# Six of nine pairs of adaLN modulations made as row dot products on VectorE, GpSimd and ScalarE

## The chip, the cores and the metric

One core of one Trainium2 chip runs the whole program once per launch. The metric is the device time of one execution in microseconds (us), the median of several runs. Three runs of the kernel before took 2188.8, 2191.82 and 2193.41 us.

## What is computed

A diffusion transformer of two layers for one image: 256 latent tokens `x` and 256 context tokens `h`, model width 1024, all float32. Each layer is a feed-forward half step, a mixer (layer 0: latent attention and a gated delta rule; layer 1: gated linear attention and windowed attention), and a second feed-forward half step. Shift, scale and gate of each of them come from the conditioning vector (adaLN): nine modulations per layer of width 1024, one set for the latents from `c`, one for the context from `c_ctx`.

```
sc, scc = silu(c), silu(c_ctx)
for i in range(2):
    mx = split(sc @ ada_w[i] + ada_b[i], 9)     # latents
    mh = split(scc @ ada_w[i] + ada_b[i], 9)    # context
    x = ffn_half_step(x, norm_g[i, 0], mx[0], mx[1], mx[2], ...)
    h = ffn_half_step(h, norm_g[i, 0], mh[0], mh[1], mh[2], ...)
    xn = modulate(rms_norm(x, norm_g[i, 1]), mx[3], mx[4])
    hn = modulate(rms_norm(h, norm_g[i, 1]), mh[3], mh[4])
    ox, oh = mixer_i(xn, hn, ...)
    x = x + mx[5] * ox
    x = ffn_half_step(x, norm_g[i, 2], mx[6], mx[7], mx[8], ...)
    if i == 0: the same for h with mh[5] to mh[8]
```

The matrices `ada_w` are 2 x 1024 x 9216 floats, 72 MB, and are used once, for two vectors. The 18 modulations are numbered m = 9 * layer + j; in layer 1 the context needs only m = 9 to 13.

## The kernel before

The tokens lie in columns: 8 tiles of 128 rows of the width by 256 tokens for each of the two sequences. Every weight block (128x1024, 512 KB) comes from DRAM through `fetch` (L216) on the SP queue into a ring of buffers `raw`; `halves` (L221) splits it into two parts of 11 bits, `whi` by a ScalarE cast (L224) and `wlo` by a VectorE subtraction with both operands in SBUF (L227), and `mm3` (L248) multiplies the three products that matter on TensorE. A feed-forward half step, `ffn` (L410), runs in four groups of 6, 6, 5 and 5 hidden tiles: for each tile a gate block and an up block of 24 matmuls each into a bank `f`, then `gated` (L464: `sg`, `ah`, `al`); at a group's end eight blocks of the down projection, whose results `add` (L475) puts onto the tokens (`x`, L405). `norm_h` (L374) makes the normed and modulated tokens (`hnf`, `hh`, `hl`) from modulations 3j and 3j + 1 of a step; the gate is needed first at group 0's end.

A pair of modulations is made by `ada` (L296). It is eight steps, one for each 128 rows of the width: two blocks of 512 KB are fetched, and four matmuls (eight records in the trace) with 32 stationary columns, of which two hold silu of `c_ctx` and `c`, run side by side into the four quarters of the bank `aux`. After the eighth step VectorE transposes the bank (`sqa`, L311) and adds the bias.

```
for q in range(2):
    r = 32 * (2 * e + q)
    self.mm(pb[r:r + 32, :], self.sc[:, k, :], raw[:, 512 * q:512 * q + 512], k == 0, k == NK - 1, cost=0.215)
```

`more_ada` (L324) does the next steps. It is called in `contexts` (L1674) before the first feed-forward step, for pair 0; in each tile of every `ffn` (L491), on that step's own ring of `raw`; and, if pairs are left, in the last mixer. All 72 steps were made within the first 1117 us.

The order of the work: streams of TensorE's work (feed-forward steps, mixer parts) are woven by their ranks (`weave`, L193) against a count of TensorE's time, and a scheduler then sets each engine's order by priority and its own estimate of when instructions are ready. Each engine executes its list in order; so does the SP queue, where a fetch waits until the block's buffer in its ring was read. The context's first step is `ffn00c`, then the latents' `ffn00x` beside the context's mixer, and so on; `ffn01x` and `ffn10x` are the latents' steps after the first mixer.

Of the kernel before, what the change touches and what calls it, by code (L numbers as in the profile page):

```python
# [83 lines left out]
def pack(i):  # L84
# [60 lines left out]
class Net:  # L145
# [75 lines left out]
    def halves(self, pool, raw, w, bufs, width=1024, ffn=False):  # L221
        """The part of 11 bits and what it leaves."""
# [40 lines left out]
    def setup(self):  # L263
# [16 lines left out]
        self.ada_gen, self.ada_pair = None, 0  # L280
# [15 lines left out]
    def ada(self, pair, pool, raws):  # L296
        """Modulations 2 pair and 2 pair + 1, one block of DRAM at each step."""
        nc = self.nc
        pb = self.bank("aux")
        for k in range(NK):  # L300
            pool, raws = self.ada_from
            for e in range(2):
                raw = self.fetch(pool, self.I["ada"][pair, k, :, 1024 * e:1024 * e + 1024], raws)
# [10 lines left out]
        for e in range(2):  # L314
            l, j = divmod(2 * pair + e, 9)
            v = self.mod[:, 2 * pair + e]
            if j % 3 == 1:
                g = self.ng[:, 3 * l + j // 3].unsqueeze(2).to_broadcast([128, NK, 2])
                nc.vector.scalar_tensor_tensor(v, v, 1.0, g, op0=ALU.add, op1=ALU.mult)
            elif j in (2, 8):  # L320
                nc.vector.tensor_scalar(v, v, 0.5, None, op0=ALU.mult)
        yield

    def more_ada(self, n, upto, pool, raws):  # L324
        """The next n blocks of the modulations' weights, no further than pair upto."""
        self.ada_from = pool, raws
        for _ in range(n):
            if self.ada_pair > min(upto, 8):
                return
# [80 lines left out]
    def ffn(self, l, j, s, side, name, rank, end=False, begin=None, raws=3, bufs=4, rows=8, tanh=False):  # L410
        """Streams of this kind share two banks: the one of lowest rank has them."""
# [21 lines left out]
        def run(ctx, pool, h):  # L433
            with ctx:
                yield 10.0
                yield from owned()
# [17 lines left out]
                def turn():  # L454
                    """Between two banks, where another stream may go first."""
# [25 lines left out]
                for lo, hi in GROUPS:  # L481
                    aT = []
                    for f in range(lo, hi):
# [6 lines left out]
                        n = NK * (f + 1) // 6 - NK * f // 6 if 2 * self.ada_pair <= gate else 1  # L490
                        self.more_ada(n, 8, pool, raws)  # L491
                        yield from turn()
                    while 2 * self.ada_pair <= gate:
                        self.more_ada(1, 8, pool, raws)
                    for k in range(0, NK, 2):
# [9 lines left out]
                        product(pb[:, N:2 * N], aT, hi - lo)  # L505
# [1222 lines left out]
```

## Time and profile before

| | |
|---|---|
| three runs | 2188.8, 2191.82, 2193.41 us |
| profiled execution: span of its instructions | 2186.0 us |
| TensorE busy / VectorE / ScalarE / GpSimd | 2102.0 / 1422.2 / 1072.3 / 241.2 us |
| `aux` matmuls of the modulations | 576 records, 111.4 us busy |
| bytes moved | 388.6 MB, mean 178 GB/s |
| first normed tile `hnf` of the context | 37.35 us |
| `ffn00c` | to 292 us |
| groups 0 and 1 of `ffn01x` | 1175 to 1281 us |

The profile was taken of one more execution; of its own time only the span from its first to its last instruction is given, 2186.0 us, 5.8 us below the median of the runs. Busy time counts an engine's instructions once where they overlap. A timeline row gives start, duration, engine, line, operation, result <- operands and shape; a bracket at its end tells how long the engine stood idle before it, and what ended that. PE is TensorE, PEld its weight loads, DVE is VectorE, ACT ScalarE, POOL GpSimd.

### The profile page before, as it was taken

Reading aid. Unit: us, or ns where it says so; the run is one execution under the profiler, and the core shown is the slowest. Engines: PE = TensorE matmul, PEld = TensorE weight load, DVE = VectorE, ACT = ScalarE, POOL = GpSimd, SP = SyncE. Lnnn points to the kernel's source line nnn. Section 1 sums busy time; section 2 is a strip of 40 time slices with the busy share of each in tenths; the row PEclk is TensorE's granted clock in tenths of the full one; section 3 lists DMA queues with packets and bytes.
Section 4 is the critical chain, followed back from the end, with each engine's and each line's share of the span. In section 5 each row is a group of like instructions: output and inputs, shape, how many; then the busy total and the mean of one; then the engine's idle time right before and its main releaser. Section 6 shows DMA issues by size and latency. Waiting matters only on the chain.

```text
span 2186.0 us, 45677 instructions
## 1 busy us (share of the span) xinstructions
PE 2102.0 (96%) x17688; PEld 1919.2 (88%) x17688; DVE 1422.2 (65%) x3153; ACT 1072.3 (49%) x2304; POOL 241.2 (11%) x496
## 2 busy tenths in 40 slices
PE   6999999999999989999998999999999998998999
PEld 2778888888898788887898999899999997878999
DVE  3545567886566878765576666766676766666665
ACT  3434456544434564444355555555555655435554
POOL 0000006601000175010000000100000001000000
PEclk8999999999999999999999999999999998999999
DMA  9867755665445645653356555555456552124554
GB/s 338 292 225 243 249 192 170 188 223 151 157 155 200 231 147 181 220 169 119 116 189 207 181 172 181 177 181 181 140 170 184 160 160 75 49 78 152 182 169 156
DMA packets 145621, 388.56 MB, mean 178 GB/s; under 512 B 32219, under 2 KB 41179, under 8 KB 145404
## 3 DMA queue, kind: packets, MB, share of 16 engines
q1 hardware_dynamic: 143920, 383.85, 54.2%
q8 instruction: 139, 2.28, 0.4%
q10 hardware_dynamic: 1484, 1.80, 0.3%
q14 instruction: 78, 0.64, 0.1%
HBM read 380.08 MB, written 5.51 MB: 176 GB/s over the span
## 4 chain that ended last, share of the span: by engine, by line
PE 77%; DMA 8%; POOL 5%; DVE 5%; ACT 2%; issue 2%; SPq 1%; DVEq 0%; ACTq 0%; POOLq 0%
PE f L175 53%; PE mm L175 11%; PE g L175 5%; DMA raw<-in_ffn 5%; PE aux L175 3%; DVE wlo L227 2%; DMA raw<-in_ada 2%; PE q L175 1%; ACT whi L224 1%; POOL tap L701 1%; PE mm L185 1%; DMA raw<-in_ev_nat 0%; PE q L185 0%; POOL vT L702 0%; DMA lout<-w 0%
## 5 line engine op out<-in xcount | busy, mean ns | idle before, releaser
L227 DVE TENSOR_TENSOR wlo<-raw,whi 128x512 fp32r<-128x512 f32 (+2 forms) x1274 | 794.0, 638 | 464.0 <-ACT whi L224 444.6
L224 ACT CAST whi<-raw 128x512 fp32r<-128x512 f32 (+2 forms) x1274 | 704.3, 571 | 752.3 <-PE f L175 413.5
L175 PE MATMUL f<-hh,whi 128*128 128x256 f32 x2464 | 707.2, 288 | 10.6 <-ACT whi L224 5.3
L175 PE MATMUL f<-hh,wlo 128*128 128x256 f32 x2464 | 704.4, 286 | 3.1 <-DVE wlo L227 3.1
L175 PE MATMUL f<-hl,whi 128*128 128x256 f32 x2464 | 702.9, 286 | 2.2 <-DVE hl L400 2.1
L175 PEld LDWEIGHTS f<-hh,whi 128*128 128x128 f32 x2464 | 474.8, 193 | 52.7 <-ACT whi L224 19.7
L175 PEld LDWEIGHTS f<-hh,wlo 128*128 128x128 f32 x2464 | 476.3, 193 | 11.6 <-DVE wlo L227 5.7
L175 PEld LDWEIGHTS f<-hl,whi 128*128 128x128 f32 x2464 | 476.2, 193 | 5.8 <-DVE hl L400 3.5
L175 PE MATMUL f<-ah,whi 128*128 128x256 f32 x1232 | 351.4, 288 | 5.1 <-DVE sg L472 2.8
L175 PE MATMUL f<-ah,wlo 128*128 128x256 f32 x1232 | 351.7, 287 | 2.5 <-DVE wlo L227 2.3
L175 PE MATMUL f<-al,whi 128*128 128x256 f32 x1232 | 350.2, 285 | 0.0
L175 PEld LDWEIGHTS f<-ah,whi 128*128 128x128 f32 x1232 | 236.7, 193 | 19.6 <-ACT whi L224 9.6
L175 PEld LDWEIGHTS f<-ah,wlo 128*128 128x128 f32 x1232 | 237.2, 193 | 9.1 <-DVE wlo L227 6.0
L175 PEld LDWEIGHTS f<-al,whi 128*128 128x128 f32 x1232 | 237.8, 193 | 0.6 <-issue 0.2
L175 PE MATMUL aux<-raw,scpad 128*32 128x512 f32 x576 | 111.4, 633 | 12.2 <-DMA raw<-in_ada 12.2
L405 DVE SCALAR_TENSOR_TENSOR x<-f,mod,x 128x256 f32<-128x256 f32 x224 | 98.2, 477 | 22.4 <-PE f L175 22.3
L175 PE MATMUL mm<-whi,hh 128*128 128x256 f32 x368 | 105.0, 299 | 4.2 <-ACT hh L395 3.8
L175 PE MATMUL mm<-wlo,hh 128*128 128x256 f32 x368 | 106.1, 292 | 0.0
L175 PE MATMUL mm<-whi,hl 128*128 128x256 f32 x368 | 103.7, 290 | 0.0
L255 ACT CAST ah<-sg 128x256 fp32r<-128x256 f32 x154 | 62.3, 405 | 63.3 <-DVE sg L469 37.2
L256 DVE TENSOR_TENSOR al<-sg,ah 128x256 fp32r<-128x256 f32 x154 | 67.1, 436 | 23.6 <-ACT ah L255 23.3
L175 PEld LDWEIGHTS mm<-whi,hh 128*128 128x128 f32 x368 | 69.7, 195 | 12.3 <-ACT hh L395 5.5
(433 smaller groups left out, 2662.7 us busy)
## 6 DMA issues: line engine op xcount, KB each, us to landing
raw<-in_ffn SPq DMA_DIRECT2D x308, 512.0 KB, 4.5
raw<-in_ada SPq DMA_DIRECT2D x144, 512.0 KB, 5.1
raw<-in_ffn SPq DMA_DIRECT2D x112, 384.0 KB, 3.3
raw<-in_ffn SPq DMA_DIRECT2D x112, 320.0 KB, 2.9
raw<-in_ev_qkv SPq DMA_DIRECT2D x24, 512.0 KB, 3.6
raw<-in_ev_nat SPq DMA_DIRECT2D x20, 512.0 KB, 5.0
raw<-in_ev_out SPq DMA_DIRECT2D x16, 512.0 KB, 4.1
raw<-in_od_k SPq DMA_DIRECT2D x32, 256.0 KB, 3.0
```

The source lines that it names most:

```text
L175: self.nc.tensor.matmul(out, lhsT=lhsT, rhs=rhs, start=start, stop=stop, **kw)
L185: self.nc.tensor.transpose(out, src, self.c["ident"][:n, :n])
L224: self.nc.scalar.copy(hi[:, :w], raw[:, :w])
L227: (self.nc.gpsimd if self.cut % P == P - 1 else self.nc.vector).tensor_tensor(lo[:, :w], raw[:, :w], hi[:, :w], op=ALU.subtract)
L255: self.nc.scalar.copy(pair[0], src)
L256: self.nc.vector.tensor_tensor(pair[1], src, pair[0], op=ALU.subtract)
L405: self.nc.vector.scalar_tensor_tensor(self.x[s][k], pb, self.mod[:, gate, k, s:s + 1], self.x[s][k], op0=ALU.mult, op1=ALU.add)
L701: nc.gpsimd.tensor_scalar(tap, raw[:, a + j - 2:b + j - 2], w[:, m, j:j + 1], None, op0=ALU.mult)
```

## The change

Pairs 0, 1, 2 and 6, 7, 8 (modulations 0 to 5 and 12 to 17) leave TensorE. Their weights now lie in DRAM turned: a block holds 128 output columns in its rows and the 1024 inputs along them. `ada_rows` first fetches silu's argument, copied to all 128 rows (`c2_rows`, 1 MB), and takes silu of it on ScalarE. Then each block needs one dot product along its rows per sequence. VectorE makes it in one instruction with an accumulator (the products go to `junk`, int8); or GpSimd multiplies into `prod`, and ScalarE copies `prod` onto itself with an accumulator. The context's dots are VectorE's, and every third of the latents' in modulations 0 and 1; the other latents' are GpSimd's and ScalarE's. The context's part of 14 to 17 is not made any more. Modulations 0 and 1 (16 blocks) are made before the first step, 2 to 5 beside `ffn00c`, on a ring of 8 blocks of their own; 12 to 17 beside `ffn01x` and `ffn10x`, on a ring of 4. Pairs 3, 4 and 5 stay on TensorE and are called after them, one step per tile and per two down blocks.

```diff
+PAIRS = (3, 6)
...
-    def ada(self, pair, pool, raws):
+    def ada(self, pair):
...
+    def ada_rows(self, pool, ms, raws):
+        nc, turn = self.nc, 0
+        sc = self.t(pool, [128, 2, D], "sc")
+        nc.sync.dma_start(out=sc, in_=self.I["c2_rows"])
+        for s in range(2):
+            nc.scalar.activation(sc[:, s], sc[:, s], AF.Silu)
+        for m in ms:
+            first = int(m > 13)
+            for t in range(NK):
+                raw = self.fetch(pool, self.I["ada_rows"][m, t], raws)
+                for s in range(first, 2):
+                    out = self.mod[:, m, t, s:s + 1]
+                    turn += s
+                    if s == 0 or m < 2 and turn % 3 == 0:
+                        junk = self.t(pool, [128, D], "junk", mybir.dt.int8, bufs=1)
+                        nc.vector.scalar_tensor_tensor(junk, raw, 1.0, sc[:, s], op0=ALU.mult, op1=ALU.mult, accum_out=out)
+                    else:
+                        prod = self.t(pool, [128, D], "prod", bufs=2)
+                        nc.gpsimd.tensor_tensor(prod, raw, sc[:, s], op=ALU.mult)
+                        nc.scalar.activation(prod, prod, AF.Copy, accum_out=out)
+                if t == NK - 1:
+                    for s in range(first, 2):
+                        v = self.mod[:, m, :, s]
+                        nc.vector.tensor_tensor(v, v, self.adab[:, m], op=ALU.add)
+                        self.ada_end(m, s, s + 1)
+                yield
...
-                        n = NK * (f + 1) // 6 - NK * f // 6 if 2 * self.ada_pair <= gate else 1
-                        self.more_ada(n, 8, pool, raws)
+                        for _ in range(1 if (gate, s) in self.ada_done else 2):
+                            next(beside, None)
                         yield from turn()
-                    while 2 * self.ada_pair <= gate:
-                        self.more_ada(1, 8, pool, raws)
+                    while (gate, s) not in self.ada_done:
+                        next(beside)
...
                         product(pb[:, N:2 * N], aT, hi - lo)
+                        next(beside, None)
...
     def contexts(self):
+        st = ExitStack()
+        rows = self.ada_rows(self.pool(st, "st", "left"), range(6), 8)
         def begin():
-            with ExitStack() as st:
-                pool = self.pool(st, "st", "left")
-                self.more_ada(2, 0, pool, 16)
-                self.load_x(0)
-                self.more_ada(NK, 0, pool, 16)
+            for step in range(2 * NK):
+                next(rows)
+                if step == 3:
+                    self.load_x(0)
+        def beside(*at):
+            yield from rows
+            st.close()
+            self.mark("rows")
+            yield from self.more_ada(*at)
...
-        self.ffn(0, 1, 1, "left", "ffn01x", 61, raws=5, bufs=6, rows=7)
-        yield "ffn01x"
-        self.ffn(1, 0, 1, "left", "ffn10x", 70, raws=5, bufs=6, rows=7)
-        yield "ffn10x"
+        with ExitStack() as st:
+            rows = self.ada_rows(self.pool(st, "st", "left"), range(2 * PAIRS[1], 18), 4)
+            self.ffn(0, 1, 1, "left", "ffn01x", 61, raws=5, bufs=6, rows=7, extra=lambda *at: rows)
+            yield "ffn01x"
+            self.ffn(1, 0, 1, "left", "ffn10x", 70, raws=5, bufs=6, rows=7, extra=lambda *at: rows)
+            yield "ffn10x"
+            for _ in rows:
+                pass
```

Since the scheduler sets the order, the change shows in the engines' lists. Between the start and the first norm, VectorE had only the transposes and biases of pair 0 to do (`sqa`), and then the norm (`hnf`, `hl`) and the first splits (`wlo`):

```order
L383 TENSOR_SCALAR nvf_228<-mm_221 128x2
L311 STREAM_TRANSPOSE sqa_213<-aux_120 128x256
L313 TENSOR_TENSOR mod_93<-sqa_213,adab_86 128x16
L311 STREAM_TRANSPOSE sqa_216<-aux_120 128x256
L313 TENSOR_TENSOR mod_93<-sqa_216,adab_86 128x16
L319 SCALAR_TENSOR_TENSOR mod_93<-mod_93,ng_88 128x16
L394 SCALAR_TENSOR_TENSOR hnf_246<-x_2_66,mod_93,mm_221 128x256
L394 SCALAR_TENSOR_TENSOR hnf_252<-x_3_67,mod_93,mm_221 128x256
L227 TENSOR_TENSOR wlo_300<-raw_297,whi_299 128x512
```

Now the dots (`junk`; `sc` is silu of the conditioning, `mod` the modulations) fill that place:

```order
L351 SCALAR_TENSOR_TENSOR junk_250,mod_93<-raw_248,sc_120 128x1024
L351 SCALAR_TENSOR_TENSOR junk_252,mod_93<-raw_248,sc_120 128x1024
L351 SCALAR_TENSOR_TENSOR junk_256,mod_93<-raw_254,sc_120 128x1024
L359 TENSOR_TENSOR mod_93<-mod_93,adab_86 128x8
L351 SCALAR_TENSOR_TENSOR junk_411,mod_93<-raw_409,sc_120 128x1024
L329 SCALAR_TENSOR_TENSOR mod_93<-mod_93,ng_88 128x8
L433 SCALAR_TENSOR_TENSOR hnf_290<-x_2_66,mod_93,mm_265 128x256
L359 TENSOR_TENSOR mod_93<-mod_93,adab_86 128x8
L433 SCALAR_TENSOR_TENSOR hnf_296<-x_3_67,mod_93,mm_265 128x256
L351 SCALAR_TENSOR_TENSOR junk_418,mod_93<-raw_416,sc_120 128x1024
```

The first `hnf` stands behind 22 dots instead of the two transposes, and the dots of modulation 2 go on between the norm's instructions.

The second place is group 1 of `ffn00c` on VectorE, around its first `sg` and `al`. Before, only splits stood there:

```order
L227 TENSOR_TENSOR wlo_1257<-raw_1254,whi_1256 128x512
L227 TENSOR_TENSOR wlo_1273<-raw_1254,whi_1272 128x512
L227 TENSOR_TENSOR wlo_1296<-raw_1293,whi_1295 128x512
L227 TENSOR_TENSOR wlo_1312<-raw_1293,whi_1311 128x512
L472 TENSOR_TENSOR sg_1288<-sg_1288,f_1169 128x256
L256 TENSOR_TENSOR al_1171<-sg_1288,ah_1170 128x256
```

Now the list there reads:

```order
L232 TENSOR_TENSOR wlo_1292<-raw_1289,whi_1291 128x512
L351 SCALAR_TENSOR_TENSOR junk_2405,mod_93<-raw_2403,sc_120 128x1024
L232 TENSOR_TENSOR wlo_1308<-raw_1289,whi_1307 128x512
L232 TENSOR_TENSOR wlo_1338<-raw_1335,whi_1337 128x512
L513 TENSOR_TENSOR sg_1284<-sg_1284,f_1167 128x256
L351 SCALAR_TENSOR_TENSOR junk_2465,mod_93<-raw_2463,sc_120 128x1024
L232 TENSOR_TENSOR wlo_1354<-raw_1335,whi_1353 128x512
L232 TENSOR_TENSOR wlo_1377<-raw_1374,whi_1376 128x512
L261 TENSOR_TENSOR al_1169<-sg_1284,ah_1168 128x256
L351 SCALAR_TENSOR_TENSOR junk_2525,mod_93<-raw_2523,sc_120 128x1024
L232 TENSOR_TENSOR wlo_1393<-raw_1374,whi_1392 128x512
```

`junk_2525` is the last of the 53 dots of the first six modulations: the scheduler has drawn all of them ahead of the second tile of group 1, though the program's text spreads them to the end of group 2. The counts up to it are 53 `junk`, 43 `wlo` of 512 and 8 of 256 elements, 50 others of 128x256, and some 20 small ones.

The third place is the SP queue in group 0 of `ffn01x`. Before, only the feed-forward's blocks were fetched there. Now blocks of the two kinds alternate:

```order
L223 DMA raw_15199<-in_ffn 128x1024
L223 DMA raw_15914<-in_ada_rows 128x1024
L223 DMA raw_15243<-in_ffn 128x1024
L223 DMA raw_15997<-in_ada_rows 128x1024
L223 DMA raw_15282<-in_ffn 128x1024
```

Of the 48 blocks of modulations 12 to 17, nine stand in the queue ahead of the first block of `ffn01x` and the last one among the down blocks of its group 1.

## Rows read from the trace of the kernel before

**Rows 1.** The page's part 1: busy us, share of the span, instructions

```profile
PE 2102.0 (96%) x17688; PEld 1919.2 (88%) x17688; DVE 1422.2 (65%) x3153; ACT 1072.3 (49%) x2304; POOL 241.2 (11%) x496
```

**Rows 2.** The page's part 4: shares of the chain that ended last, by line

```profile
PE f L175 53%; PE mm L175 11%; PE g L175 5%; DMA raw<-in_ffn 5%; PE aux L175 3%; DVE wlo L227 2%; DMA raw<-in_ada 2%; PE q L175 1%; ACT whi L224 1%; POOL tap L701 1%; PE mm L185 1%; DMA raw<-in_ev_nat 0%; PE q L185 0%; POOL vT L702 0%; DMA lout<-w 0%
```

**Rows 3.** Windows: length, busy PE, PEld, DVE, ACT, POOL, PE clock, DMA share, GB/s

```profile
0.00:38.00 38.00, 21.46 (x80) 4.74 (x80) 4.55 (x14) 6.04 (x13) 2.94 (x17) 0.91 0.93 333
38.00:123.00 85.00, 81.32 (x596) 66.89 (x597) 54.66 (x116) 41.64 (x88) 3.06 (x12) 0.96 0.84 293
123.00:292.00 169.00, 160.50 (x1221) 138.89 (x1220) 83.61 (x173) 68.72 (x143) 0.00 (x0) 0.97 0.69 231
292.00:1117.00 825.00, 802.44 (x7453) 701.82 (x7453) 579.08 (x1371) 398.32 (x918) 191.13 (x331) 0.99 0.54 175
1117.00:1175.00 58.00, 51.98 (x409) 49.80 (x406) 43.51 (x97) 32.04 (x69) 4.40 (x12) 0.94 0.63 219
1175.00:1281.00 106.00, 105.98 (x883) 105.78 (x883) 66.25 (x124) 55.80 (x108) 0.00 (x0) 1.00 0.58 184
```

**Rows 4.** Timeline of POOL and DVE at 375 and 396 us, pairs put together

```profile
374.95 1.23 POOL L912 TENSOR_TENSOR w<-gg,const 128x512 f32<-128x512 f32 x1
...
375.20 1.26 DVE L706 SCALAR_TENSOR_TENSOR kT<-cv,kT 128x256 f32<-128x256 f32 x1
...
395.80 0.73 POOL L702 TENSOR_TENSOR qT<-qT,tap 128x255 f32<-128x255 f32 x1
...
396.01 1.06 DVE L227 TENSOR_TENSOR wlo<-raw,whi 128x512 fp32r<-128x512 f32 x1
...
397.17 0.93 POOL L701 TENSOR_SCALAR tap<-cv,ev_conv 128x254 f32<-128x254 f32 x1
...
397.70 0.41 DVE L227 TENSOR_TENSOR wlo<-raw,whi 128x256 fp32r<-128x256 f32 x1
```

**Rows 5.** GpSimd's two-input lines: count, ns least/median/most, first and last start

```profile
L702 POOL TENSOR_TENSOR qT<-qT,tap x16: 718/734/1185, 374.3 to 829.1; 128x254 f32<-128x254 f32 x8, 128x255 f32<-128x255 f32 x8
...
L913 POOL TENSOR_TENSOR M<-gN,const x8: 1037/1043/1489, 368.4 to 814.7; 128x512 f32<-128x512 f32 x8
...
L1109 POOL TENSOR_TENSOR w<-w,gtmp x3: 1290/1664/1686, 619.9 to 1087.8; 128x512 f32<-128x512 f32 x3
```

**Rows 6.** Timeline of DVE: two operands in SBUF, GpSimd not in the way

```profile
38.14 1.29 DVE L227 TENSOR_TENSOR wlo<-raw,whi 128x512 fp32r<-128x512 f32 x2
...
369.42 0.43 DVE L706 SCALAR_TENSOR_TENSOR qT<-cv,qT 128x256 f32<-128x256 f32 x1 [0.98 <-ACT cv L705]
```

**Rows 7.** ScalarE at 512 elements, with an accumulator, as in rows 5

```profile
L588 ACT ACTIVATE P<-aux,smr,qss1r x3: 772/774/779, 1895.9 to 1928.4; 128x512 f32<-128x512 f32 x3
```

**Rows 8.** Timeline of PE: a modulation step between dense matmuls

```profile
157.76 0.28 PE L175 MATMUL f<-hh,wlo 128*128 128x256 f32 x1
157.97 1.06 PE L175 MATMUL aux<-raw,scpad 128*32 128x512 f32 x8
```

**Rows 9.** Windows of `aux` matmuls alone: length, busy PE (records), clock, DMA

```profile
0.00:38.00 38.00, 19.22 (x64) 0.91 0.93 333
38.00:123.00 85.00, 14.03 (x72) 0.96 0.84 293
123.00:292.00 169.00, 21.23 (x136) 0.97 0.69 231
292.00:1117.00 825.00, 56.29 (x302) 0.99 0.54 175
```

**Rows 10.** Timeline of DVE: first two tiles of group 1 of `ffn00c`

```profile
119.17 0.42 DVE L472 TENSOR_TENSOR sg<-sg,f 128x256 f32<-128x256 f32 x1 [0.63 <-ACT sg L471]
...
126.86 0.41 DVE L472 TENSOR_TENSOR sg<-sg,f 128x256 f32<-128x256 f32 x1
```

**Rows 11.** Timeline of the start: first weight block, first norm

```profile
6.92 3.15 PE L175 MATMUL aux<-raw,scpad 128*32 128x512 f32 x8 [6.92 <-DMA raw<-in_ada]
...
37.35 0.87 DVE L394 SCALAR_TENSOR_TENSOR hnf<-x,mod,mm 128x256 f32<-128x256 f32 x2
```

More of the change, by code (lines that the diff above doesn't have):

```diff
@@ L90, in pack @@
     out["c2"] = c2.reshape(NK, 128, 2).transpose(1, 0, 2)
+    out["c2_rows"] = np.broadcast_to(np.stack([f["c_ctx"], f["c"][0]]), (128, 2, D))
     out["ada_b"] = f["ada_b"].reshape(18, NK, 128).transpose(2, 0, 1)
@@ L314, in ada @@
         for e in range(2):
[L315 to L321, printed above, removed]
-        yield
[L324 to L329, printed above, removed]
+            self.ada_end(2 * pair + e, 0, 2)
@@ new lines, in ada, with ada_end @@
+        yield
+    def ada_end(self, m, a, b):
+        nc, (l, j), v = self.nc, divmod(m, 9), self.mod[:, m, :, a:b]
+        if j % 3 == 1:
+            g = self.ng[:, 3 * l + j // 3].unsqueeze(2).to_broadcast([128, NK, b - a])
+            nc.vector.scalar_tensor_tensor(v, v, 1.0, g, op0=ALU.add, op1=ALU.mult)
+        elif j in (2, 8):
+            nc.vector.tensor_scalar(v, v, 0.5, None, op0=ALU.mult)
+        self.ada_done |= {(m, s) for s in range(a, b)}
+    def ada_rows(self, pool, ms, raws):
[24 more added lines that the diff above has]
+                yield
@@ L330, in more_ada @@
+    def more_ada(self, pool, raws):
+        while self.ada_pair < PAIRS[1]:
+            self.ada_from = pool, raws
             if self.ada_gen is None:
-                self.ada_gen, self.ada_k = self.ada(self.ada_pair, pool, raws), 0
+                self.ada_gen, self.ada_k = self.ada(self.ada_pair), 0
             next(self.ada_gen)
@@ L376, in norm_h @@
         nc = self.nc
+        assert self.ada_done.issuperset({(9 * l + 3 * j + e, s) for e in range(2)}), (l, j, s)
         pb = self.bank(bank or tag)
@@ L407, in residual, with ffn @@
             self.sumsq(k, s)
-    def ffn(self, l, j, s, side, name, rank, end=False, begin=None, raws=3, bufs=4, rows=8, tanh=False):
+    def ffn(self, l, j, s, side, name, rank, end=False, begin=None, raws=3, bufs=4, rows=8, tanh=False, extra=None):
         nc = self.nc
@@ L437, in run @@
                 at, late = 0, []
+                beside = extra(pool, raws) if extra else iter(())
                 def product(out, acts, n):
@@ L1328, in dense @@
             self.mark("end")
-        def modulations():
-            while self.ada_pair < 9:
-                self.more_ada(1, 8, pl, 2)
-                yield 0
-            self.mark("ada")
         def attention():
@@ L1339, in attention @@
             self.lanes([self.swa_rows(h, t, ("f", "f", "aux")[(2 * h + t) % 3]) for h in range(8) for t in range(2)], 2, rank + 4)
-        self.start(modulations(), 90)
         self.start(self.gla_latents(self.pg), rank)
@@ L1674, in contexts @@
     def contexts(self):
+        st = ExitStack()
+        rows = self.ada_rows(self.pool(st, "st", "left"), range(6), 8)
         def begin():
-            with ExitStack() as st:
-                pool = self.pool(st, "st", "left")
-                self.more_ada(2, 0, pool, 16)
-                self.load_x(0)
-                self.more_ada(NK, 0, pool, 16)
-        self.ffn(0, 0, 0, "right", "ffn00c", 50, begin=begin, raws=5, bufs=5, rows=6)
+            for step in range(2 * NK):
[7 more added lines that the diff above has]
+            yield from self.more_ada(*at)
+        self.ffn(0, 0, 0, "right", "ffn00c", 50, begin=begin, raws=5, bufs=5, rows=6, extra=beside)
         yield "ffn00c"
@@ L1686, in contexts @@
         yield "endm00"
-        self.ffn(0, 1, 0, "right", "ffn01c", 80, raws=4, bufs=4, rows=6, tanh=True)
+        self.ffn(0, 1, 0, "right", "ffn01c", 80, raws=4, bufs=4, rows=6, tanh=True, extra=self.more_ada)
         yield "ffn01c"
@@ L1698, in latents @@
         Mixer0.consts(self)
-        self.ffn(0, 0, 1, "left", "ffn00x", 60, raws=4, bufs=4, rows=6, tanh=True)
+        yield "rows"
+        self.ffn(0, 0, 1, "left", "ffn00x", 60, raws=4, bufs=4, rows=6, tanh=True, extra=self.more_ada)
         yield "ffn00x"
```

10 lines of the change are left out of this document (6 added, 4 removed).

## Prediction

> **What bounds the kernel now.** I read the page's busy times first: TensorE (PE) is busy 96% of the span, VectorE (DVE) 65%, GpSimd (POOL) 11% [rows 1]. Then the chain that ended last: TensorE's own lines hold most of it, the modulations' matmuls (`aux`) 3%, and the waits for their weights 2% [rows 2]. So in the middle of the program a removed microsecond of TensorE is a saved one. But the change takes work from TensorE only to lay it on engines that feed TensorE, so the question is where these stand. The table by stage tells it [rows 3]: until 38 us the DMA engines bound (0.93 of them busy, 333 GB/s); from 38 to 123 us VectorE is busy 55 of 85 us; in the feed-forward step of the latents after the first mixer (`ffn01x`, from 1175 us) 66 of 106. There is free time on VectorE, but it is less than half of the span, and it has to hold GpSimd's work too, if the two get in each other's way.
>
> They do. Where GpSimd runs a two-input TENSOR_TENSOR, a VectorE instruction with two SBUF operands that starts meanwhile stands still until 0.13 us before GpSimd's end, and then takes its usual time. In [rows 4] GpSimd's `qT` runs from 395.80 to 396.53; `wlo` starts at 396.01 and takes 1.06 us instead of 0.68, as if begun at 396.39. GpSimd's `w` ends at 376.18; `kT` starts at 375.20 and takes 1.26 instead of 0.43, as if begun at 376.03. There are 26 such pairs between 345 and 865 us, and in every one the wait ends 0.12 to 0.20 us before GpSimd does. The other way round GpSimd waits too: its `qT` line goes from 0.718 us to 1.185 [rows 5]. So the two exclude each other, but for VectorE's instructions that read PSUM and one SBUF operand.
>
> **Prices.** *A dot on VectorE* (`junk`, 128x1024, both operands in SBUF): 256 elements take 0.43 us, two back-to-back of 512 take 1.29 [rows 6]. By the slope 1024 cost 0.645 + 2 x 0.215 = 1.08, by doubling 1.29; I take 1.2. *A product on GpSimd* (`prod`, 128x1024): the median is 0.734 at 254 elements and 1.043 at 512 (`M`, one operand a constant), by that slope 1.66 at 1024; `w` of L1109, with two whole tensors of 512, takes at least 1.29, doubled 2.58 [rows 5]. The operation is that of the first, the operands those of the second: I take the middle, 2.05, of which 1.92 keep VectorE out. [...] *The sum on ScalarE* (`prod` in place): 0.774 us at 512 [rows 7], so up to 1.6 at 1024; 91 of them are at most 146 us on an engine that is busy half of the span [rows 1], in its own queue behind GpSimd; it costs nothing as long as GpSimd, with 2.05 each, is the slower of the two, and if it were not, GpSimd would wait for one of its two `prod` buffers. *A step removed from TensorE* (8 records): 1.15 us where it stands between dense matmuls, from the end of the slot of 157.76 to 159.03 [rows 8]; by busy time 21.23/17 = 1.25 between 123 and 292 us and 56.29/37.75 = 1.49 later [rows 9]. I take 1.25, with 1.15 and 1.49 as ends.
>
> **The change, place by place.** 48 of 72 steps leave TensorE. In their place come 160 dots: 69 on VectorE (48 for the context and 5 for the latents in the first six modulations, 16 in 12 and 13), 91 on GpSimd and ScalarE (43 and 48). The bytes stay, but for two tables of silu's argument of 1 MB each.
>
> *From the start to the first gates of group 1.* In the order of VectorE all 53 dots of the first six modulations stand ahead of the second `al` of group 1 of `ffn00c`; before, that point was passed between 119 and 127 us, say 123 [rows 10]. Up to the last dot VectorE now has 53 dots x 1.2 = 64 us, 43 `wlo` of 512 x 0.645 = 28, 8 of 256 and 50 others of 256 x 0.4 = 23, 20 small x 0.15 = 3: 117 us. A block is fetched only when the block 8 before it has been read by both engines, so when VectorE makes its 48th block, GpSimd has finished 40, of which 5 were VectorE's alone: 35 x 1.92 = 67 us in which VectorE's two-operand work stands still. Some 25 of VectorE's instructions here (`hnf`, `sg`, `x`) read PSUM and can run beside GpSimd: 10 us, of which I give back 8. The first dot can begin at about 9 us: today's first block lands at 6.9 [rows 11], and the table of 1 MB and two ScalarE passes over 1024 elements go ahead of it. 9 + 117 + 67 - 8 = 185 instead of 123: **+62 us**. TensorE has 63 us of feed-forward work in that time (8 pairs of blocks of 48 matmuls and 144 of group 0's down products, 0.12 us apart [rows 8]), so it waits. What is late in the start is the norm: all first 16 blocks go ahead of `hnf`, which began at 37.35 [rows 11]; 9 + 22 dots x 1.2 + 15 other x 0.5 + 11 x 1.92 give 64 us at most for it.
>
> *After that, to the end of the mixers.* Of the 72 steps 8 lay before 38 us and 9 before 123 [rows 9], 55 after. Now 24 come after. 31 x 1.25 = **-39 us**, since TensorE bounds there (160.5 of 169 and 802 of 825 us busy [rows 3]). Nothing is added to that stretch.
>
> *`ffn01x`, and the end of the mixer before it.* 48 blocks more, on a ring of 4 in the same SP queue as the feed-forward's blocks: 9 stand ahead of `ffn01x`, 39 among its groups 0 and 1, so that group 1 can't be fetched to its end before GpSimd has done nearly all. VectorE's 66 us of the 106 [rows 3] + 7 dots x 1.2 + 39 x 1.92 = 149, less 28 PSUM readers of 0.43 (12): 137, so +31. The 9 ahead meet 43.5 of 58 busy us [rows 3]: 43.5 + 9 x (1.2 + 1.92) = 72, at most +14; TensorE has other streams there, I take +6. Together **+37 us**. `ffn10x` and what follows have nothing to wait for.
>
> The sum is 62 - 39 + 37 = +60, made against the profiled execution and its span of 2186.0 us. The median of the three runs is 5.8 us above that span, so 2191.8 + 60 = **2252 us**. With the low ends (1.53 kept from VectorE, a dot at 1.08, all PSUM readers beside GpSimd, 1.49 a step) the three terms are +41, -46 and +16: 2203. With the high ends (2.45, 1.29, next to no overlap, 1.15 a step) +91, -36 and +74: 2321.
>
> **The rivals.** *VectorE's free time takes it all: faster.* Between 38 and 292 us VectorE is idle 116 of 254 us [rows 3]; GpSimd's 43 products need 83. If they ran in the gaps in which VectorE waits for ScalarE or TensorE anyway, nothing would be late: VectorE's 117 us from 9 us on end at 126, about where they end today, group 0 and 1 of `ffn01x` stay, and the -39 us stand alone: about 2153. It decides at the hold: under GpSimd's one-input `tap` VectorE is hardly kept (`wlo` of 397.70 stands in the midst of the `tap` of 397.17 and takes its 0.41 us [rows 4]), and at a hold of 0.25 us 35 products would cost 9 us. Against it: `prod` has two inputs, and the order lets the dots run together at the front instead of in the gaps. 12%.
>
> [...]
>
> *It cancels.* If half of the holds fall into waits that VectorE has anyway, the two added terms shrink to about the 39 us saved: 2187 to 2197. 6%.
>
> That the change doesn't do what it says I can exclude: TensorE's order keeps 24 steps, and none before the first feed-forward block.
>
> **How the numbers follow.** The exclusion at the prices above has 75%, its own range is 2203 to 2321. The faster case has 12%, the half rate 7%, the cancelling 6%. About 0.2% (4 us) is what a measurement of this kernel can tell from no change. Faster by more: the 12% and a third of the cancelling, 14%; within it 6%, the rest of the cancelling and the lowest edge of the likeliest; slower 80%. The range of 2192 to 2318 holds nearly all of the likeliest case and half of the cancelling one; left out are the faster case and the half rate.
>
> **What would show it.** In the new profile: `junk` near 1.2 us where GpSimd rests and 2 to 3 us where it runs; `prod` near 2 us; the first `hnf` at 55 to 65 us instead of 37; the second `sg` of group 1 near 185; TensorE's busy share down in the first 200 us and again at the start of `ffn01x`, waiting for `wlo`; 192 `aux` records instead of 576; the stretch from there to the first mixer's end shorter by some 39 us. I am wrong if `wlo` keeps its 0.70 us mean while `prod` runs, or if the first `hnf` comes before 45 us.

## The result, and the profile after

The changed kernel takes **2314.84 us** (four runs, 2311.45 to 2316.01) against 2190.31 for the kernel before on the same chip (2186.97 to 2193.41): a ratio of **1.058, 95% interval 1.055 to 1.060**, 124 us slower. The forecast was 2252 us, slower by 60. The sign and the range held; the forecast loss is half of the measured one.

The page of the changed kernel, the busy times and the chain that ended last [rows 1, 2]:

```profile
span 2314.2 us, 45434 instructions
...
PE 2066.4 (89%) x17304; PEld 1945.9 (84%) x17304; DVE 1659.6 (72%) x3291; ACT 1169.7 (51%) x2490; POOL 498.6 (22%) x587
...
PE 70%; DVE 13%; issue 5%; DMA 5%; POOL 4%; ACT 3%; SPq 0%; DVEq 0%; ACTq 0%; POOLq 0%
```

TensorE lost 36 us of work and 7 points of share. The chain holds 13% of VectorE and 4% of GpSimd now. The windows tell in which stretches TensorE rests (length, then busy PE, PEld, DVE, ACT, POOL, PE clock, DMA share, GB/s) [rows 3]:

```profile
0.00:38.00 38.00, 2.72 (x12) 2.64 (x12) 27.25 (x32) 15.24 (x28) 21.40 (x15) 1.00 0.95 353
38.00:64.00 26.00, 3.94 (x16) 3.56 (x16) 24.14 (x30) 7.78 (x17) 20.77 (x15) 1.00 0.65 230
64.00:123.00 59.00, 29.40 (x146) 26.64 (x147) 58.93 (x70) 24.46 (x47) 46.47 (x25) 0.91 0.47 159
123.00:185.00 62.00, 45.53 (x289) 43.72 (x288) 61.20 (x70) 32.11 (x66) 39.94 (x15) 0.81 0.57 195
...
364.00:777.00 413.00, 404.53 (x3812) 367.45 (x3812) 294.86 (x697) 208.00 (x485) 88.85 (x159) 0.98 0.52 170
777.00:1180.00 403.00, 387.09 (x3637) 357.51 (x3635) 291.71 (x695) 202.47 (x456) 99.11 (x172) 0.96 0.43 132
1180.00:1238.00 58.00, 21.14 (x144) 19.87 (x142) 50.88 (x66) 26.88 (x53) 34.38 (x21) 0.66 0.64 238
1238.00:1410.00 172.00, 128.36 (x927) 124.01 (x928) 145.50 (x164) 95.69 (x193) 97.14 (x41) 0.85 0.65 224
1410.00:1500.00 90.00, 88.69 (x738) 88.28 (x738) 58.77 (x121) 48.34 (x105) 4.60 (x12) 1.00 0.53 171
```

There are two holes, and both are where GpSimd's products run: to 185 us TensorE is busy 82 of 185 us while VectorE is full from 64 us on (59 of 59, 61 of 62); from 1180 to 1410 us it is busy 150 of 230. In between and behind, nothing is lost: from the first gate of `ffn01x`'s group 2 to the end it is 904 us, and was 905. TensorE's mean granted clock is down to 0.81 from 123 to 185 us and to 0.66 from 1180 to 1238; what that adds to the loss was not tried apart.

The parts of a dot, from the tile views (count; minimum/median/maximum in ns):

```profile
L351 DVE SCALAR_TENSOR_TENSOR junk<-raw,sc x69: 1208/1215/3440, 9.0 to 1253.3; 128x1024 int8<-128x1024 f32 x69
L351 DVE DVE_READ_ACCUMULATOR junk<-raw,sc x69: 73/77/83, 10.1 to 1256.7; 128x1 f32 x69
...
L354 POOL TENSOR_TENSOR prod<-raw,sc x91: 2331/2591/3488, 10.0 to 1381.6; 128x1024 f32<-128x1024 f32 x91
L355 ACT ACTIVATE prod<-prod x91: 1038/1053/1062, 12.4 to 1390.1; 128x1024 f32<-128x1024 f32 x91
```

A dot is 1.21 us at rest and up to 3.44; a product never takes less than 2.33. How the two meet is in the timeline of VectorE and GpSimd (start, duration, engine, line):

```profile
80.44 1.21 DVE L351 SCALAR_TENSOR_TENSOR junk<-raw,sc 128x1024 int8<-128x1024 f32 x1
...
81.58 0.86 DVE L433 SCALAR_TENSOR_TENSOR hnf<-x,mod,mm 128x256 f32<-128x256 f32 x2
82.36 2.59 DVE L351 SCALAR_TENSOR_TENSOR junk<-raw,sc 128x1024 int8<-128x1024 f32 x1
...
84.88 0.68 DVE L232 TENSOR_TENSOR wlo<-raw,whi 128x512 fp32r<-128x512 f32 x1
85.49 2.56 DVE L439 SCALAR_TENSOR_TENSOR hl<-hnf,mod,hh 128x256 fp32r<-128x256 f32 x1
...
80.52 3.34 POOL L354 TENSOR_TENSOR prod<-raw,sc 128x1024 f32<-128x1024 f32 x1
83.95 1.08 POOL L394 TENSOR_SCALAR nrf<-nrf 128x2 f32<-128x2 f32 x1
85.00 2.76 POOL L354 TENSOR_TENSOR prod<-raw,sc 128x1024 f32<-128x1024 f32 x1
```

The product that is issued at 80.52 waits for the dot that runs to 81.65, and takes 3.34 instead of 2.33. Within it the two `hnf`, which read PSUM, take their usual time (0.86 us, before 0.87 [rows 11]), and the dot of 82.36 stands until the product is nearly over, as if begun at 83.74. Over the whole trace 76 of VectorE's `wlo`, `al`, `hl`, `acc` and `junk` begin within a product: all 76 are held, to 0.13 to 0.20 us before its end. Of the 18 `hnf`, `sg` and `x` that do, none is.

### The profile page after: what moved, and what is told of

It is laid out like the page before. It is cut to its first block, busy times and chain, and to the rows that moved or that the text cites. A ratio compares the mean times of both kernels' runs of the same rounds, so it can differ in the third digit from the quotient of the medians.

```text
span 2314.2 us, 45434 instructions
## 1 busy us (share of the span) xinstructions
PE 2066.4 (89%) x17304; PEld 1945.9 (84%) x17304; DVE 1659.6 (72%) x3291; ACT 1169.7 (51%) x2490; POOL 498.6 (22%) x587
## 4 chain that ended last, share of the span: by engine, by line
PE 70%; DVE 13%; issue 5%; DMA 5%; POOL 4%; ACT 3%; SPq 0%; DVEq 0%; ACTq 0%; POOLq 0%
PE f L180 50%; PE mm L180 9%; PE g L180 5%; DVE wlo L232 5%; DMA raw<-in_ffn 3%; DVE junk L351 2%; PE aux L180 1%; ACT whi L229 1%; PE q L180 1%; DVE acc L408 1%; DVE hl L439 1%; PE mm L190 1%; DVE al L261 1%; DVE mod L359 1%; POOL prod L354 1%
## 5 line engine op out<-in xcount | busy, mean ns | idle before, releaser
L232 DVE TENSOR_TENSOR wlo<-raw,whi 128x512 fp32r<-128x512 f32 (+3 forms) x1274 | 876.9, 703 | 386.8 <-ACT whi L229 366.5
L229 ACT CAST whi<-raw 128x512 fp32r<-128x512 f32 (+3 forms) x1274 | 706.2, 570 | 693.0 <-PE f L180 463.0
L180 PE MATMUL f<-hl,whi 128*128 128x256 f32 x2464 | 716.1, 291 | 29.0 <-DVE hl L439 28.9
L180 PE MATMUL f<-hh,wlo 128*128 128x256 f32 x2464 | 713.1, 290 | 15.4 <-DVE wlo L232 15.3
L180 PEld LDWEIGHTS f<-hh,whi 128*128 128x128 f32 x2464 | 483.5, 197 | 44.7 <-DVE sg L513 15.9
L180 PEld LDWEIGHTS f<-hl,whi 128*128 128x128 f32 x2464 | 484.7, 197 | 35.6 <-DVE hl L439 33.8
L180 PEld LDWEIGHTS f<-hh,wlo 128*128 128x128 f32 x2464 | 484.8, 197 | 20.6 <-DVE wlo L232 18.3
L354 POOL TENSOR_TENSOR prod<-raw,sc 128x1024 f32<-128x1024 f32 x91 | 247.1, 2730 | 149.0 <-ACT prod L355 99.6
L351 DVE SCALAR_TENSOR_TENSOR junk<-raw,sc 128x1024 int8<-128x1024 f32 x69 | 108.7, 1575 | 13.3 <-ACT sc L341 9.5
L355 ACT ACTIVATE prod<-prod 128x1024 f32<-128x1024 f32 x91 | 95.7, 1052 | 39.0 <-POOL prod L354 39.0
L260 ACT CAST ah<-sg 128x256 fp32r<-128x256 f32 x154 | 62.2, 404 | 89.9 <-DVE sg L513 69.6
```

Of the source, the lines that this page charges most:

```text
L180: self.nc.tensor.matmul(out, lhsT=lhsT, rhs=rhs, start=start, stop=stop, **kw)
L229: self.nc.scalar.copy(hi[:, :w], raw[:, :w])
L232: (self.nc.gpsimd if self.cut % P == P - 1 else self.nc.vector).tensor_tensor(lo[:, :w], raw[:, :w], hi[:, :w], op=ALU.subtract)
L260: self.nc.scalar.copy(pair[0], src)
L351: nc.vector.scalar_tensor_tensor(junk, raw, 1.0, sc[:, s], op0=ALU.mult, op1=ALU.mult, accum_out=out)
L354: nc.gpsimd.tensor_tensor(prod, raw, sc[:, s], op=ALU.mult)
```

## The experiments

**Theory A**: GpSimd's two-input products and VectorE's two-SBUF work exclude each other, and what is queued behind the products on GpSimd (the norms' small inverse square root, 12 instructions in the trace) is late with them. **Rival B**: VectorE's own 69 dots, and that they stand so early in the order, cost the time. **Rival C**: ScalarE's sums do.

Four marks are read from each run's trace, as the start of the instruction, in us: the second gate of group 1 of `ffn00c` (the product of `sg`), the norm of `ffn01x` (`nvf`), the first gate of its group 2, and the span. Times are medians, ratios the 95% intervals of those to the kernel before on the same chip. The kernel before took 2182.7 to 2184.1 there in the runs from e1 on (2190.3 beside the changed kernel), so what lies between two runs is worked out from their ratios, 1% being 21.8 us.

| run | gate | norm | group 2 | span | time | ratio |
|---|---|---|---|---|---|---|
| before | 126.9 | 1159.1 | 1280.9 | 2186.0 | 2190.3 | |
| after | 211.7 | 1221.9 | 1410.1 | 2314.2 | 2314.8 | 1.055 to 1.060 |
| e1_vector_dots | 135.3 | 1132.4 | 1265.9 | 2173.5 | 2178.4 | 0.997 to 1.000 |
| e2_no_products | 132.6 | 1130.6 | 1257.6 | 2160.4 | 2165.6 | 0.990 to 0.994 |
| e3_first_only | 211.0 | 1230.3 | 1352.8 | 2256.2 | 2260.5 | 1.032 to 1.039 |
| e4_last_only | 144.2 | 1159.5 | 1346.8 | 2251.3 | 2254.3 | 1.030 to 1.036 |
| e5_last_vector | 144.1 | 1150.0 | 1282.5 | 2188.9 | 2187.2 | 1.001 to 1.004 |
| e6_rsqrt_vector | 213.0 | 1211.8 | 1388.6 | 2289.7 | 2289.8 | 1.047 to 1.051 |
| e7_short_dots | 171.4 | 1174.4 | 1351.3 | 2256.1 | 2257.0 | 1.032 to 1.037 |
| e8_one_input | 142.7 | 1146.2 | 1301.0 | 2205.5 | 2207.6 | 1.009 to 1.013 |
| e13_one_input_rsqrt | 144.7 | 1142.3 | 1272.5 | 2174.2 | 2177.9 | 0.996 to 0.999 |
| e9_nine_rows | 135.9 | 1165.9 | 1298.0 | 2206.4 | 2206.6 | 1.008 to 1.012 |
| e10_pair0_pe | 114.7 | 1115.5 | 1249.5 | 2157.5 | 2158.0 | 0.986 to 0.990 |
| e11_spread | 135.4 | 1137.6 | 1270.5 | 2177.0 | 2178.0 | 0.996 to 0.999 |
| e12_both | 117.2 | 1115.6 | 1248.7 | 2156.5 | 2158.3 | 0.987 to 0.990 |

### All dots on VectorE

```
-                    if s == 0 or m < 2 and turn % 3 == 0:
+                    if True:
```

> All 160 row dots on VectorE; no product on GpSimd and no sum of one on ScalarE. Theory A (a GpSimd product of 2.33 us or more holds VectorE's instructions with two SBUF operands, and the norm's small GpSimd steps queue behind the products): each of the 91 products (2.33 at the least, 2.73 mean) is replaced by a dot of 1.21 plus 0.07, so faster than the changed kernel by about 91 x 1.0 to 1.4 us where VectorE is the bound, less what TensorE hides: 2210 to 2250 us. Second gate of group 1 of ffn00c near 180 us instead of 212, the norm's small GpSimd steps of ffn01x done within 5 us instead of 16, mean of VectorE's 512-column wlo back to about 0.70. Rival B (GpSimd was hidden; VectorE's own dots and their early place cost the time): 91 x 1.28 us more on VectorE, 2380 us or more. Rival C (ScalarE's 1.05 us sums are what is waited for): faster too, but the wlo mean as in the changed kernel (0.76).

The ratio falls from 1.0576 to 0.9987, 129 us, more than A had asked for, and B falls: with 91 dots more VectorE is busy 74 us *less*. The page of this run:

```profile
PE 2037.3 (94%) x17304; PEld 1918.3 (88%) x17304; DVE 1585.7 (73%) x3473; ACT 1079.0 (50%) x2308; POOL 253.1 (12%) x496
```

My estimate of the gate (near 180) was too late for two reasons: this order puts 64 dots, not 96, ahead of that gate, and nothing is held there. The mean of the 512-column `wlo` is back, 697 ns against 764 in the changed kernel (lines by form), which speaks against C:

```profile
L232 DVE TENSOR_TENSOR wlo<-raw,whi 128x512 fp32r<-128x512 f32 x1036 | 712.9, 697 | 293.0 <-ACT whi L229 280.6 <-PE f L180 4.8
```

### The products left out

```
-                        nc.gpsimd.tensor_tensor(prod, raw, sc[:, s], op=ALU.mult)
-                        nc.scalar.activation(prod, prod, AF.Copy, accum_out=out)
+                        nc.scalar.activation(prod, raw, AF.Copy, accum_out=out)
```

> The multiplications of the 91 GpSimd products are left out (ScalarE sums the raw block itself), so these 91 dots are not dots; all else stays. Theory A: the hold of 35 x 2.2 = 77 us leaves the front and up to 56 x 2.2 = 123 us leaves ffn01x and the tail of the mixer ahead of it, of which 95 us was visible: second gate of group 1 near 135 us, the whole near 2150 to 2190 us. Rival B (VectorE's 69 dots and the order cost the time): within 20 us of the changed kernel's 2315. Rival C (ScalarE's sums): within 20 us of 2315 too, since the sums stay.

2165.6, as A said, and the gate at 132.6 where some 135 was expected. The 69 dots stay with all 53 of the first six modulations ahead of that gate, and so do ScalarE's 91 sums: B and C are out, both would have left the time near 2315. The whole loss, and a gain of 0.8% behind it, hang on GpSimd's 91 multiplications.

### Either end alone

```
-PAIRS = (3, 6)
+PAIRS = (3, 9)
...
-            rows = self.ada_rows(self.pool(st, "st", "left"), range(2 * PAIRS[1], 18), 4)
```

> Only pairs 0 to 2 as row dots at the front; pairs 3 to 8 as TensorE steps. If the three stretches add up (front +85 us at the second gate of group 1, 24 steps of about 1.25 us less later, and nothing after ffn01c): second gate at 212 us as in the changed kernel, whole near 2190 + 85 - 25 = 2250 us. If the tail's and ffn01x's +95 us come from something earlier (clock, a shifted order): near 2315.

```
-PAIRS = (3, 6)
+PAIRS = (0, 6)
...
-        rows = self.ada_rows(self.pool(st, "st", "left"), range(6), 8)
```

> Pairs 0 to 5 as TensorE steps, pair 0 ahead of the work as before, and only pairs 6 to 8 as row dots from ffn01x on. If the stretches add up: 2190 + 95 (tail of the mixer and ffn01x) - 24 x 1.25 (steps gone) = 2255 us, with the second gate of group 1 near 127 us and the norm's small GpSimd steps of ffn01x again slow (16 us). If ffn01x's loss needs the earlier part: near 2165.

2260 (2250 expected) and 2254 (2255): each hole comes without the other. `ffn01x` alone, from norm to group 2, takes 187.3 us with no row dot before the mixer's tail, 188.2 in the changed kernel, 121.8 before. The first `hnf` there comes 21.8 us after `nvf`, as in the changed kernel (21.9; before 6.9). The gate of this second run came at 144 us, not at 127; the next run has it too.

### The last three pairs on VectorE

The last run, with `if True:` as in the first.

> As the run with only pairs 6 to 8 as row dots, but all 64 of these dots on VectorE. If GpSimd's hold is the whole of what that run lost (2254 against 2184 us): the 64 dots take 64 x 1.29 = 83 us on VectorE beside ffn01x and ffn10x, where VectorE has room, and 24 TensorE steps of about 1.25 us go: 2155 to 2175 us, faster than the kernel before. If the dots on VectorE beside ffn01x cost what they take: 2184 - 30 + 83 = 2237 us.

Between the two prices: 67 us better than with products, but 0.2% over the kernel before. `ffn01x` takes 132.5 us against 121.8, so dots of 1.3 (55 of the 64 stand there) cost 11; `ffn00c`, where the pace of the TensorE steps is now that of the changed kernel, passes its second gate 17 us later than before, and of the 30 us that 24 fewer steps should give 9 are left at `ffn01x`'s norm.

### The norms' inverse square root on VectorE

```
-        self.rsqrt(y, v, 2, tag, nc.vector if tag in '' else None)
+        self.rsqrt(y, v, 2, tag, nc.vector)
```

> The changed kernel, with the small inverse square root of the feed-forward blocks' norms on VectorE (10 small instructions) instead of GpSimd (13). If the queueing of these steps behind the products is a cost of its own: about 16 us sooner at the first product of ffn01x (first hnf of ffn01x 7 us after its nvf instead of 22) and some of it at the front, so 2285 to 2300 us. If the stretch is set by the products' sum alone (48 x 2.4 us on GpSimd and the hold on VectorE), the time saved is waited for elsewhere: 2310 to 2320 us.

The ratio falls to 1.0491, 19 us (the profiled span 24), within the first expectation, but only half of it comes from the queue. The gate stays, the norm comes 10 us sooner, the norm to group 2 is 11 shorter. The 11 are the queue's: from `nvf` to the first `hnf` of `ffn01x` it is 10.4 us instead of 21.9 (7 was expected), and from that `hnf` to group 2 166.4 as against 166.3. The 10 are not: TensorE's 9000th matmul (those of the modulations left out) starts at 1172.1 us instead of 1181.6, ahead of the first of these products (1183.6 and 1192.4). What gained them inside the mixer, where no product runs, stays open. So the queue on GpSimd is a cost of its own, some 11 us here. (The trace has 12 of these instructions on GpSimd and 9 on VectorE, not 13 and 10.) GpSimd's timeline in the changed kernel shows it:

```profile
1224.22 0.51 POOL L381 TENSOR_SCALAR nrf<-nvf 128x2 int32<-128x2 int32 x1
1224.81 2.69 POOL L354 TENSOR_TENSOR prod<-raw,sc 128x1024 f32<-128x1024 f32 x1
...
1233.97 2.34 POOL L354 TENSOR_TENSOR prod<-raw,sc 128x1024 f32<-128x1024 f32 x1
1236.27 1.18 POOL L393 TENSOR_TENSOR nrf<-nrf 128x2 f32<-128x2 f32 x1
1237.40 2.33 POOL L354 TENSOR_TENSOR prod<-raw,sc 128x1024 f32<-128x1024 f32 x1
1239.82 0.21 POOL L394 TENSOR_SCALAR nrf<-nrf 128x2 f32<-128x2 f32 x1
1240.00 2.34 POOL L354 TENSOR_TENSOR prod<-raw,sc 128x1024 f32<-128x1024 f32 x1
1242.30 0.19 POOL L395 TENSOR_TENSOR nyf<-nrf 128x2 f32<-128x2 f32 x1
```

Five of the 12 small steps start right behind a product of another stream, and some are stretched to 1.2 us beside VectorE's dots. In TensorE's waits from 1180 to 1410 us (us in all, times, longest) this is one row, TensorE standing for the norm; the other three are waits for VectorE's late work:

```profile
PE mm L426 <- POOL nyf L395: 20.7, 1, 20.7
PE f L180 <- DVE sg L513: 17.4, 5, 7.2
PE f L180 <- DVE hl L439: 12.5, 5, 4.1
...
PE f L180 <- DVE wlo L232: 8.1, 7, 1.8
```

### Short dots

```
-                        nc.vector.scalar_tensor_tensor(junk, raw, 1.0, sc[:, s], ...
+                        nc.vector.scalar_tensor_tensor(junk[:, 0:64], raw[:, 0:64], 1.0, sc[:, s, 0:64], ...
```

> VectorE's 69 dots taken over 64 of their 1024 columns only (so they are not the dots), all else as in the changed kernel, GpSimd's 91 products in full. Theory A (hold by the products): VectorE is freed of 53 x 1.1 = 58 us at the front and 16 x 1.1 = 18 us later, but GpSimd's products run as before and set the end there: first hnf somewhat sooner, second gate of group 1 at 160 to 200 us, whole 2255 to 2300 us. Rival B (the VectorE dots are the cost): the whole loss at the front goes, 2315 - 85 = 2230 us or less.

Within A's bounds. 69 dots shortened by 1.0 us give 51 us (1.0576 to 1.0341): VectorE was full, so most of a dot's time is paid, but 74 us of the loss stay without them.

### One input instead of two

```
-                        nc.gpsimd.tensor_tensor(prod, raw, sc[:, s], op=ALU.mult)
+                        nc.gpsimd.tensor_scalar(prod, raw, 1.0, None, op0=ALU.mult)
```

> GpSimd's 91 products read one input instead of two (the block times the constant 1, so these are not the dots); GpSimd stays as long in use, or nearly (1.0 to 2.3 us each), and ScalarE's sums and the release of the blocks stay. If what costs is that a two-input GpSimd instruction excludes VectorE's two-input ones: 2165 to 2200 us, with VectorE's 512-column wlo back at a mean of 0.70. If what costs is GpSimd's lateness (blocks freed late, norm's steps queued): within 30 us of 2315.

The sharpest of the runs: GpSimd is *longer* at each product, 2.77 us, and the kernel is 102 us faster (1.0576 to 1.0111). It ends 8 us over A's range, and `wlo`'s mean is 0.72, not quite the 0.70 expected. The tile view, and then the timelines of VectorE and GpSimd:

```profile
L354 POOL TENSOR_SCALAR prod<-raw x91: 2763/2775/3843, 8.2 to 1298.6; 128x1024 f32<-128x1024 f32 x91
```

```profile
120.86 1.85 DVE L232 TENSOR_TENSOR wlo<-raw,whi 128x512 fp32r<-128x512 f32 x2
122.64 1.21 DVE L351 SCALAR_TENSOR_TENSOR junk<-raw,sc 128x1024 int8<-128x1024 f32 x1
...
123.78 0.68 DVE L232 TENSOR_TENSOR wlo<-raw,whi 128x512 fp32r<-128x512 f32 x1
...
121.32 2.85 POOL L354 TENSOR_SCALAR prod<-raw 128x1024 f32<-128x1024 f32 x1 [0.32 <-ACT prod L355]
```

The dot of 122.64 and the `wlo` of 123.78 begin within the product of 121.32 to 124.17 and take their usual time; the `wlo` pair of 120.86, in its beginning, takes 1.85 us, where two of 512 at rest take 1.29 [rows 6]. Of some 200 such VectorE instructions that begin within a product some 70 are held, each until about 1.9 us before the product's end, which is the first 0.9 us of a product of 2.77. (The scheduler also moved some dots: 46 instead of 53 stand ahead of the gate, and 31 products instead of 43. So the 102 us need not be the hold alone; the run without products has as many ahead of the gate as the changed kernel, and bounds it.)

### One input, and the root on VectorE

Both edits above together.

> As the run with one-input GpSimd products (so the 91 dots are not dots), and the norms' small inverse square root on VectorE as in the run that moved it. In the one-input run 37 us lay between ffn01x's nvf and its first hnf (7 in the kernel before, 22 in the changed kernel). If what the one-input run still lost (2207.6 against 2165.6 without any product) is the wait of the norms' small GpSimd steps behind long products: about 25 to 35 us come back, 2173 to 2183 us, and nvf to first hnf in ffn01x within 10 us. If it is the blocks that GpSimd frees late, or what GpSimd still holds of VectorE: 2195 to 2210 us.

29 us come back (1.0111 to 0.9977), and `nvf` to the first `hnf` in `ffn01x` falls from 37 us to 7. With one-input products the small steps had stood behind a product each, eleven in a row:

```profile
1176.06 0.20 POOL L393 TENSOR_TENSOR nrf<-nrf 128x2 f32<-128x2 f32 x1
1176.22 2.77 POOL L354 TENSOR_SCALAR prod<-raw 128x1024 f32<-128x1024 f32 x1
1178.96 0.22 POOL L394 TENSOR_SCALAR nrf<-nrf 128x2 f32<-128x2 f32 x1
1179.14 2.77 POOL L354 TENSOR_SCALAR prod<-raw 128x1024 f32<-128x1024 f32 x1
1181.88 0.19 POOL L395 TENSOR_TENSOR nyf<-nrf 128x2 f32<-128x2 f32 x1
```

What remains to the run without products (0.9921) is 12 us. So of the 143 us between the changed kernel and that run, 102 go with the second input, although the norm's wait grew from 22 to 37 us with it; 29 go with the small steps behind the products once the second input is gone (some 11 with it there); 12 with the rest. What of these is blocks freed late and what the hold of 0.9 us was not tried apart. GpSimd's wait for ScalarE to give back a `prod` buffer (92.6 us in this run, 99.6 in the changed kernel) is still there, so it can hardly cost more than these 12.

### A version that beats both

Pair 0 stays on TensorE ahead of the work as in the kernel before; pairs 1, 2 and 6 to 8 are dots, all on VectorE (part of the edit):

```
-PAIRS = (3, 6)
+PAIRS = (0, 6)
...
-        rows = self.ada_rows(self.pool(st, "st", "left"), range(6), 8)
+            rows.append(self.ada_rows(self.pool(st, "st", "left"), range(2, 6), 8))
...
-                    if s == 0 or m < 2 and turn % 3 == 0:
+                    if True:
```

> Search for a version that beats both. As the run with all dots on VectorE, but pair 0, on which the first norm waits, stays on TensorE ahead of the work as in the kernel before (32 dots fewer, 8 TensorE steps more). In the all-VectorE run the first hnf came at 57 us (before 37) and the second gate of group 1 at 135 (before 127). If the 32 dots ahead of the first norm are what is late there: first hnf near 37 us, second gate of group 1 near 115 to 127, whole about 10 to 20 us below the all-VectorE run, 2160 to 2170 us. If the front is bound by VectorE's sum up to the gate of m2 or by the transfers: within 5 us of 2178.

**2158.0 us, 0.988 of the kernel before (0.986 to 0.990)**, even under the expected range. The first `hnf` is back at 35.0, the gate at 114.7. The front's windows:

```profile
0.00:38.00 38.00, 22.23 (x83) 6.04 (x84) 6.86 (x18) 8.38 (x18) 2.91 (x17) 0.90 0.94 340
38.00:123.00 85.00, 80.03 (x627) 78.43 (x627) 83.04 (x167) 43.79 (x88) 7.98 (x12) 0.95 0.89 322
123.00:273.00 150.00, 146.20 (x1098) 125.97 (x1097) 121.72 (x254) 69.96 (x146) 0.24 (x1) 1.00 0.74 257
```

TensorE is busy 80 of 85 us while VectorE is full with dots in its former gaps: the free time that one of the rivals had counted on is there, once nothing holds it.

Two edits looked for more:

```
+            def sparse():
+                for _ in rows:
+                    yield
+                    yield
```

> As the run with all dots on VectorE, but the dots of pairs 6 to 8 are spread over ffn01x and ffn10x (a step at every second place) instead of a step at each place. From ffn01x's norm to the next norms the all-VectorE run took 218 us against 205.5 before, with 64 dots there. If dots lying close together bind VectorE there: about half of these 12 us come back, 2165 to 2173 us. If each dot costs where it lies: no change, 2178.

> Both of the two edits above together: if both gain, 2150 to 2165 us; if neither, 2178.

Spreading the last 64 dots changes nothing, alone (2178.0) or with the other (2158.3).

All nine pairs on VectorE (pairs 3 to 5 beside `ffn00x` and `ffn01c`, with rings of 3 instead of 4):

> All nine pairs as row dots on VectorE (pairs 3 to 5 beside ffn00x and ffn01c, whose rings shrink from 4 blocks to 3 and from 4 halves to 3 to make room): 48 dots more on VectorE (61 us) in a stretch where TensorE is the bound, 24 TensorE steps of about 1.25 us fewer. If the dots are hidden there: 2150 to 2165 us. If they are not, or if the smaller rings cost: 2180 to 2230 us.

2206.6. The front is that of the all-VectorE run, `ffn00c` ends 23 us sooner without TensorE's steps, but `ffn01x`'s norm comes 34 us later. Whether the dots or the smaller rings cost that, this run doesn't tell.

## Why the prediction had the cause and half of the size

The mechanism was the one that it gave 75%. What failed is the sum: it made the hold of GpSimd's products too small in all three places, and it put the norm's small steps on GpSimd, which wait among those products, at nothing. Three terms, on the marks of the profiled executions:

| stretch | forecast | measured |
|---|---|---|
| start to the second gate of group 1 | +62 | +85 |
| from there to `ffn01x`'s norm (-39, and +6 for the mixer's tail) | -33 | -22 |
| `ffn01x`'s norm to its group 2 | +31 | +66 |

*The front, +62: the hold was mis-sized.* The step was 35 products at 2.05, 1.92 of it kept from VectorE, less 8 for PSUM readers: 59. A product takes 2.33 at the least, and all 43 products lie ahead of that gate, not 35. Counted on the trace (each VectorE instruction against the usual time of its kind), 82 us are held: 23 more, which is the whole miss. The other parts of the sum stood: VectorE busy 198.5 us from 9 to 212, less 82, leaves 116.5 (117 forecast); the dot was 1.21 (1.2). The first `hnf` came at 69.6; 64 had been called the most. Of my rows, `w` of whole tensors, doubled to 2.58 [rows 5], was nearer to the 2.33 than my middle of 2.05.

*To `ffn01x`'s norm, -33.* Two errors partly cancel here. Up to TensorE's 9000th matmul (modulations left out) the changed kernel is 48 us shorter than the kernel before, where -39 was forecast; that all 48 are the steps' is not shown. From there to the norm, the mixer's tail, it takes 40.3 us against 14.2: +26, where +6 was taken. The runs agree on this tail: 40.3 too with only the last three pairs as dots, 26 to 29 with these dots on VectorE, with one input or without products. So the two-input products cost 11 to 14 us of the 26; the rest comes with the dots and their blocks, or the order, and was not tried apart.

*`ffn01x`, +31: the hold mis-sized, and a wait missing.* "`ffn10x` and what follows have nothing to wait for" was right. Of the 66 us, 51 lie between the first `hnf` and group 2 (166.3 against 114.9). They are the hold: they stay with the small root moved (166.4) and go with one input (117.6) or no product (120.5). The sum had 31: it counted 63 us of hold (39 x 1.92 less 12), the trace some 75, and VectorE, which it took as busy all through, is idle 30 of the 188 us. The other 15 lie between `nvf` and the first `hnf` (21.9 against 6.9) and were not in the sum. I had counted what GpSimd's products hold on VectorE, and what GpSimd waits for, but not what else GpSimd does in that stretch: 12 instructions of the norm, in its queue among products, with TensorE waiting at their end. [Rows 3] show GpSimd's 4.40 us there before, and I read them as nothing. (With one input the whole stretch falls by 33 us, 188.2 to 154.8, which only looks like the 31: 49 go with the hold, and the norm's wait grows by 15. With the root moved as well it is 130.2.)

*The rivals.* The half rate of an accumulating dot, to which the prediction gives 7%, falls. No run shows it: 1024 elements with an accumulator take 1.21 us and 77 ns more to read it, where my estimate from [rows 6] without one is 1.08 to 1.29. That VectorE's free time takes it all is false for these products and true for dots on VectorE alone. The sums on ScalarE cost nothing in the run without products, where they stay; but GpSimd did wait for them, 99.6 us for its `prod` buffers, a wait that the prediction expected only if ScalarE were the slower of the two.

*What would show it.* `junk` 1.2 and up to 3.4, 192 `aux` records, TensorE's hole at the front and the `wlo` mean (0.70 to 0.76) came as said; `prod` (2.33, not near 2), the first `hnf` (69.6, not 55 to 65) and the second gate (212, not 185) came later. In the second hole TensorE waited less for `wlo` than for `sg`, `hl` and the norm's root.

## What to carry to other kernels

In this kernel, work moved to GpSimd with two SBUF inputs did not add to VectorE's time but took it away: 91 products of 2.33 us cost 129 us more than the same 91 dots of 1.3 us on VectorE itself. Before giving an idle engine long instructions, list every short one in its queue and who waits for it; a chain of 12 small steps among products of another stream turned 7 us into 22. Where the moved work stands ahead of the first use, leave the first piece where it was: that alone took the all-VectorE version from 2178 to 2158 us.

## What was not expected of the hardware

A one-input multiplication of 128x1024 took GpSimd longer than a two-input one (2.76 against 2.33 us at the least), and kept VectorE's two-SBUF instructions out only in its first 0.9 us. The two-input product kept out all that began within it (76 of 76 held, to 0.13 to 0.20 us before its end), the one-input product some 70 of 200.
